# Parts of two norms issued at other products, between mixer 1 and the last feed-forward block

## The chip, the cores and the metric

The kernel runs on one core of a Trainium2 chip. The metric is the device time of one execution in microseconds (us), lower is better. The median of three runs before the change is 2760.47 us (2759.29 to 2761.58).

The engines of the core are PE (TensorE, matrix products; its weight loads are listed apart as PEld), DVE (VectorE), ACT (ScalarE), POOL (GpSimd) and SP (SyncE, which here only issues transfers). Each works through its own queue of instructions in order.

## The reference

A two-layer backbone over 512 latent tokens and 256 context tokens, model width 1024. Each layer is a half feed-forward block, a token mixer, and another half feed-forward block; each block is modulated, gated and closed by a layer norm:

```python
def layer_norm(x, g, b):
    xf = x.astype(jnp.float32)
    mu = jnp.mean(xf, axis=-1, keepdims=True)
    var = jnp.mean(jnp.square(xf - mu), axis=-1, keepdims=True)
    return ((xf - mu) * lax.rsqrt(var + LN_EPS)).astype(x.dtype) * g + b
...
def swiglu(u, w_in, w_out):
    a, v = jnp.split(u @ w_in, 2, axis=-1)
    return (jax.nn.silu(a) * v) @ w_out
...
        h_lat = layer_norm(ALPHA * h_lat + m_lat[5] * y_lat, ln_g[i, 1], ln_b[i, 1])

        h_lat = ffn_sublayer(h_lat, m_lat[6], m_lat[7], m_lat[8], ffn_w_in[i, 1], ffn_w_out[i, 1], ln_g[i, 2], ln_b[i, 2])
```

The last two statements, in layer 1 (the second layer), are the place of this change: `y_lat` is the output of mixer 1 (windowed attention), the norm behind it is called `l4` in the kernel, and the feed-forward block behind that is called "1b". Context tokens are no longer computed there. The output of "1b" is the result.

## The kernel before

**Data.** Activations lie transposed: eight tiles `z[d]` of 128 channels by 512 tokens (tile 0 in `zspare` for a while). In this part of the program the tokens are worked in two groups of 256, group 0 (tokens 0 to 255) and group 1. Weights come from DRAM in float32 tiles `wr` (128x512), one transfer each on SP's queue. Products are exact to float32: a tile is split in a high part (`wh` by an ACT cast, L102; `uh`, `gh`, `woh` for activations) and a low part (`wl` by a POOL subtraction, L104; `ul`, `gl`, `wol`), and each product is three matmuls: high by high (L163), low by high (L165), high by low (L166).

**A norm.** `layer_norm` (L428 on) makes five parts: sums (adds the eight tiles on DVE L347 and on POOL, called `asl`, with DVE's running sum in the PSUM tile `pml`), mean (a matmul by a matrix of ones into `pml`, L442), centers (eight DVE subtractions, L364, then eight squares on ACT, L451, and their sums on DVE and POOL, L347), variance (four small matmuls into `pvl`, L467, then on DVE an addition, L472, the seed of a reciprocal root, L354, and three Newton steps of three operations each, L357 to L359, that end in `yl`) and spreading (PE matmuls that spread `yl` over the tile, into `prl`, L395). Behind them come the outputs: per tile the norm itself (DVE, L480), then the modulated input of the next block, `ufl` (ACT L317), its high part `uh` (ACT L319) and low part `ul` (DVE L322). Last, "kept": POOL scales each tile for the residual (L335). So `l4[g]` is the list [sums, mean, centers, variance, spreading, outputs, kept] of group g.

**Products around it.** `wo_pairs` (L828) makes mixer 1's output products `pow`, eight tiles d per group, each evacuated by one DVE operation, z[d] += gate times product (`accumulate`, L495). The names `pow3_1_256_d` are those of the last head pairs' product for group 1. In `ffn` the first chunk of "1b" makes per group four products: `pa1b_0`, `pv1b_0`, `pa1b_1`, `pv1b_1` (each 8 tiles x 3 matmuls), a gate on each pair (`sl1b`, Silu on ACT, L522; times `pv1b` on DVE, L523; high part `gh1b` on ACT, L524; low part `gl1b` on DVE, L525), and then the eight down products `pd1b_0..7`, each 6 matmuls, each again evacuated by L495. All this is done for group 0 and then for group 1. Group 0's first products need the outputs of `l4[0]`; the norm of group 1 is done while group 0's products run. Behind this chunk come further chunks (with sums `x1b` of activations, L563), and at the end the final norm of the two groups (`layer_norm_pe`, L399: squares `sqfin` on ACT L412, sums `pvfin` on PE L414; outputs `ot` on ACT L1340 or POOL L1338, each stored by a transfer).

**Order.** A scheduler puts the instructions on each engine's queue by a modelled timeline, taking the program's own order into account. The program names points: `at("pa1b_0_0_0")` is reached just behind the code of that product, and `plan(point=[parts])` says which parts are issued there. `behind(x, y)` forces x to stand after y on the same engine; `accumulate` puts every evacuation behind `keep_back[0]`, if it is set.

## Time and profile before

| | |
|---|---|
| median of the runs | 2760.47 us |
| profiled execution | 2773.53 us |
| its span, first to last instruction | 2771.7 us |
| mean granted TensorE clock | 0.985 |
| ACT busy | 1204.9 us (43%) |
| POOL busy | 1674.3 us (60%) |
| DMA moved, mean | 113 GB/s |

The profile is of one execution, which is 13 us longer than the median of the runs. A timeline row reads: start in us, busy time in us, engine, line of the kernel, operation, outputs<-inputs, shape, how many such instructions in a row, and in brackets how long the engine had idled and which instruction released it. Buffer numbers are left out of names, so `z` can be any of tiles 1 to 7.

### The profile page before, as it was taken

To read this page: it belongs to the slowest core of one execution; us is meant where nothing else is said; L and a number is where in the kernel's file an instruction comes from. 1 tells how busy PE (TensorE), PEld (TensorE's weight loads), DVE (VectorE), ACT (ScalarE), POOL (GpSimd) and SP (SyncE) were. 2 spreads that over 40 slices of the span, in tenths; PEclk is the share of its full clock that TensorE was granted. 3 is DMA by queue.
4 is the path that set the end of the run, shared out by engine and by line. 5 is a ranking of instruction groups with operands and counts; after the bars stand their busy time and mean duration, and the time that the engine had idled before them with its cause. 6 is when DMAs were issued, how large, how long until landed. Compare 5 with 4: busy or idle time off the path is not lost. (4 is left out here: it accounts for less than half of the span.)

```text
span 2771.7 us, 47917 instructions
## 1 busy us (share of the span) xinstructions
PE 2659.9 (96%) x16954; PEld 2423.5 (87%) x16954; DVE 1857.4 (67%) x4250; ACT 1204.9 (43%) x2493; POOL 1674.3 (60%) x1522
## 2 busy tenths in 40 slices
PE   8999999999999989999999999999998999899997
PEld 5899998888888889999998899999986777898997
DVE  4877777775555677656565776666587667677765
ACT  5334343366446344343433434343336655444442
POOL 4786765464434556867664577767545445667762
PEclk9999999999999999999999999999998999999998
DMA  9367555422222213444453236465722111235551
GB/s 320 105 174 205 143 155 152 144 80 61 58 58 57 63 46 92 117 127 126 125 132 106 73 87 165 112 166 165 205 87 63 32 31 47 63 103 126 133 143 57
DMA packets 295615, 311.92 MB, mean 113 GB/s; under 512 B 27856, under 2 KB 193872, under 8 KB 294352
## 3 DMA queue, kind: packets, MB, share of 16 engines
q1 hardware_dynamic: 278960, 279.36, 33.8%
q0 software_dynamic: 16128, 29.37, 6.3%
q8 instruction: 134, 2.20, 0.3%
q14 instruction: 105, 0.86, 0.1%
q10 hardware_dynamic: 288, 0.14, 0.0%
HBM read 300.92 MB, written 12.25 MB: 113 GB/s over the span
## 5 line engine op out<-in xcount | busy, mean ns | idle before, releaser
L104 POOL TENSOR_TENSOR wl<-wr,wh 128x512 fp32r<-128x512 f32 x200 | 262.7, 1332 | 161.2 <-ACT wh L102 102.7
L104 POOL TENSOR_TENSOR wl_s<-S,wh_s 128x512 fp32r<-128x512 f32 x240 | 316.6, 1354 | 53.5 <-ACT wh_s L102 53.0
L102 ACT CAST wh_s<-S 128x512 fp32r<-128x512 f32 x256 | 155.9, 620 | 430.3 <-POOL S L636 151.2
L636 POOL TENSOR_TENSOR S<-wr,wr 128x512 f32<-128x512 f32 x128 | 173.6, 1356 | 191.8 <-DMA wr<-in_wst_dram 177.5
L211 DVE CUSTOM_DVE_ANT_0 jk<-wt,cb 128x512 f32<-128x512 f32 x360 | 244.5, 679 | 23.7 <-DMA wt<-in_wmodt_dram 18.9
L104 POOL TENSOR_TENSOR wl_a<-wr,wh_a 128x512 fp32r<-128x512 f32 x144 | 189.5, 1364 | 17.9 <-ACT wh_a L102 14.0
L102 ACT CAST wh_a<-wr 128x512 fp32r<-128x512 f32 x192 | 118.9, 622 | 152.8 <-PE pd1b L165 21.8
L102 ACT CAST wh<-wr 128x512 fp32r<-128x512 f32 x200 | 120.3, 617 | 85.5 <-DMA wr<-in_wst_dram 21.9
L495 DVE SCALAR_TENSOR_TENSOR z<-pd0b,gt,z 128x256 f32<-128x256 f32 (+1 forms) x168 | 97.0, 594 | 43.9 <-PE pd0b L166 43.2
L495 DVE SCALAR_TENSOR_TENSOR z<-pd1a,gt,z 128x512 f32<-128x512 f32 (+1 forms) x160 | 95.5, 613 | 39.1 <-PE pd1a L166 38.5
L912 POOL TENSOR_SCALAR p<-p,l 128x512 f32<-128x512 f32 x64 | 44.5, 697 | 110.0 <-DVE l L1020 107.5
L495 DVE SCALAR_TENSOR_TENSOR z<-pd0a,gt,z 128x512 f32<-128x512 f32 (+1 forms) x160 | 93.4, 611 | 16.5 <-PE pd0a L166 16.3
L335 POOL TENSOR_SCALAR z<-z,ag_None,ab_None 128x256 f32<-128x256 f32 (+1 forms) x78 | 62.7, 807 | 63.7 <-DVE uh L321 48.8
L636 POOL TENSOR_TENSOR S<-wr,S 128x512 f32<-128x512 f32 x64 | 90.4, 1413 | 3.5
L636 POOL TENSOR_TENSOR S<-S,wr 128x512 f32<-128x512 f32 x64 | 90.3, 1411 | 2.9
L912 POOL TENSOR_SCALAR pw<-pw,l 128x512 f32<-128x512 f32 (+1 forms) x64 | 41.2, 643 | 66.7 <-DVE l L1214 25.7
L1019 ACT ACTIVATE p<-s,m 128x512 f32<-128x512 f32 x64 | 44.0, 689 | 81.2 <-DVE m L1017 76.5
L317 ACT ACTIVATE ufl<-z,bi_None,sc_None 128x256 f32<-128x256 f32 (+1 forms) x86 | 55.3, 654 | 52.9 <-DVE z L480 51.8
L322 DVE TENSOR_TENSOR ul<-ufl,uh 128x256 fp32r<-128x256 f32 (+1 forms) x88 | 61.0, 699 | 5.1 <-ACT uh L319 3.6
L495 DVE SCALAR_TENSOR_TENSOR z<-pd1b,gt,z 128x512 f32<-128x512 f32 (+1 forms) x91 | 53.2, 618 | 11.2 <-PE pd1b L166 10.4
L211 DVE CUSTOM_DVE_ANT_0 jk<-zspare,cb 128x512 f32<-128x512 f32 x88 | 59.7, 678 | 0.5
L163 PE MATMUL vn<-wh,uh 128*128 128x256 f32 x192 | 54.9, 286 | 1.0 <-DVE nq L856 0.5
(1483 smaller groups left out, 10650.8 us busy)
## 6 DMA issues: line engine op xcount, KB each, us to landing
wr<-in_wst_dram SPq DMA_DIRECT2D x456, 256.0 KB
wt<-in_wmodt_dram SPq DMA_DIRECT2D x206, 256.0 KB
zspare<-in_wmodt_dram SPq DMA_DIRECT2D x50, 256.0 KB
wr_0b<-in_wst_dram SPq DMA_DIRECT2D x47, 256.0 KB
wr_1b<-in_wst_dram SPq DMA_DIRECT2D x47, 256.0 KB
wr_2b<-in_wst_dram SPq DMA_DIRECT2D x47, 256.0 KB
wr_3b<-in_wst_dram SPq DMA_DIRECT2D x47, 256.0 KB
wm<-in_wmod_dram SPq DMA_DIRECT2D x8, 1024.0 KB
```

The lines of the kernel that those rows point to most:

```text
L102: nc.scalar.copy(hi[:], src[:])
L104: x = eng.tensor_tensor(out=lo[:], in0=src[:], in1=hi[:].bitcast(F32), op=ALU.subtract)
L163: behind(nc.tensor.matmul(ps, a[0], b[0], start=first, stop=False), in_front[0])
L211: x = nc.vector.tensor_tensor_reduce(out=junk[:], in0=w[:], in1=cb[st], scale=1.0, scalar=0.0, op0=ALU.mult, op1=ALU.add, accum_out=out[st])
L317: nc.scalar.activation(uf[:, :n], zs, AF.Identity, scale=s1, bias=s2)
L322: return hi, nc.vector.tensor_tensor(out=lo, in0=uv, in1=uo.bitcast(F32), op=ALU.subtract)
L335: nc.gpsimd.tensor_scalar(out=zs, in0=zs, scalar1=prm[2][:, d:d + 1], scalar2=prm[3][:, d:d + 1], op0=ALU.mult, op1=ALU.add)
L495: last[0] = nc.vector.scalar_tensor_tensor(out=zt(d, c0, c1), in0=pd, scalar=gt[:, d, st:st + 1], in1=zt(d, c0, c1), op0=ALU.mult, op1=ALU ...
L636: nc.gpsimd.tensor_tensor(out=t[:], in0=a[:], in1=b[:], op=o)
L912: nc.gpsimd.tensor_scalar(out=p, in0=p, scalar1=r, scalar2=0.0, op0=ALU.mult, op1=ALU.add)
L1019: last_exp[0] = nc.scalar.activation(p[:], ps[:], AF.Exp, bias=m[:, 0:1], scale=-1.0, accum_out=l[:, 0:1])
```

## The change

No instruction is added or removed. Three things are edited:

1. The helper `back`, which sets `keep_back[0]`, moves out of `ffn` to the outer level.
2. When the variance of `l4[0]` has been issued (point `wo7_3`), `keep_back` is set to the last instruction of its Newton steps, and it is cleared again at point `pow3_1_256_2`. So the evacuations of products 0, 1 and 2 of group 1's last output products are forced behind the Newton steps of group 0's norm.
3. In the norm of group 1, mean and centers move from the point `pv1b_0_0_0` to `pa1b_0_0_0` (one product sooner, behind "kept" of group 0); variance moves from the down product 3 to `pv1b_0_1_0` (the last product ahead of the down products); spreading, outputs and "kept" move from down product 7 to down product 3.

```diff
     last_rstd, last_add, hold, keep_back = [None], [None], [None], [None]
+
+    def back(x):
+        keep_back[0] = x
...
-        def back(x):
-            keep_back[0] = x
...
-    plan(wo6_2=l4[0][:1], wo6_3=l4[0][1:2], wm7_3=l4[0][2:3], wo7_3=l4[0][3:4], pow3_1_256_2=l4[0][4:6],
-         pow3_1_256_7=l4[1][:1])
+    plan(wo6_2=l4[0][:1], wo6_3=l4[0][1:2], wm7_3=l4[0][2:3], wo7_3=l4[0][3:4] + [lambda: back(last_rstd[0])],
+         pow3_1_256_2=[lambda: back(None)] + l4[0][4:6], pow3_1_256_7=l4[1][:1])
     wa_mixer(gate(1, 5, 1.0))
-    plan(pa1b_0_0_0=l4[0][6:], pv1b_0_0_0=l4[1][1:3], pd1b_0_0_3=l4[1][3:4], pd1b_0_0_7=l4[1][4:])
+    plan(pa1b_0_0_0=l4[0][6:] + l4[1][1:3], pv1b_0_1_0=l4[1][3:4], pd1b_0_0_3=l4[1][4:])
     ffn("1b", g1, lambda: gate(1, 8, 0.5), None, final, apart=True)
```

Lines of the changed kernel behind L345 are 3 higher than before as far as L813, and 1 higher from there on; the rows below carry each kernel's own.

What the scheduler makes of it is seen in three places. First DVE's queue around the Newton steps of the first norm. A row is line, operation, output<-inputs, shape; `pow_1_256_d` is output product d of group 1. Before, from the second Newton step on (one step's start and an evacuation stand just ahead):

```order
L357 TENSOR_TENSOR pvl_0_26140<-pvl_0_26140,yl_0_26144 128x2
L495 SCALAR_TENSOR_TENSOR z_94<-pow_1_256_3_26235,gt_5_22846,z_94 128x256
L495 SCALAR_TENSOR_TENSOR z_95<-pow_1_256_4_26243,gt_5_22846,z_95 128x256
L358 SCALAR_TENSOR_TENSOR pvl_0_26140<-pvl_0_26140,yl_0_26144 128x2
L495 SCALAR_TENSOR_TENSOR z_96<-pow_1_256_5_26251,gt_5_22846,z_96 128x256
L359 SCALAR_TENSOR_TENSOR yl_0_26144<-pvl_0_26140,yl_0_26144 128x2
L495 SCALAR_TENSOR_TENSOR z_97<-pow_1_256_6_26259,gt_5_22846,z_97 128x256
L357 TENSOR_TENSOR pvl_0_26140<-pvl_0_26140,yl_0_26144 128x2
L358 SCALAR_TENSOR_TENSOR pvl_0_26140<-pvl_0_26140,yl_0_26144 128x2
L495 SCALAR_TENSOR_TENSOR z_98<-pow_1_256_7_26267,gt_5_22846,z_98 128x256
L359 SCALAR_TENSOR_TENSOR yl_0_26144<-pvl_0_26140,yl_0_26144 128x2
L347 TENSOR_TENSOR pml_1_26275<-z_95,z_96 128x256
```

and with the change:

```order
L360 TENSOR_TENSOR pvl_0_26140<-pvl_0_26140,yl_0_26144 128x2
L361 SCALAR_TENSOR_TENSOR pvl_0_26140<-pvl_0_26140,yl_0_26144 128x2
L498 SCALAR_TENSOR_TENSOR z_94<-pow_1_256_3_26235,gt_5_22846,z_94 128x256
L362 SCALAR_TENSOR_TENSOR yl_0_26144<-pvl_0_26140,yl_0_26144 128x2
L360 TENSOR_TENSOR pvl_0_26140<-pvl_0_26140,yl_0_26144 128x2
L361 SCALAR_TENSOR_TENSOR pvl_0_26140<-pvl_0_26140,yl_0_26144 128x2
L362 SCALAR_TENSOR_TENSOR yl_0_26144<-pvl_0_26140,yl_0_26144 128x2
L498 SCALAR_TENSOR_TENSOR zspare<-pow_1_256_0_26158,gt_5_22846,zspare 128x256
L498 SCALAR_TENSOR_TENSOR z_92<-pow_1_256_1_26166,gt_5_22846,z_92 128x256
L498 SCALAR_TENSOR_TENSOR z_93<-pow_1_256_2_26174,gt_5_22846,z_93 128x256
L498 SCALAR_TENSOR_TENSOR z_96<-pow_1_256_5_26251,gt_5_22846,z_96 128x256
L483 TENSOR_TENSOR zspare<-zspare,prl_0_26182 128x256
```

The three steps stand together, with only the evacuation of product 3 among them; products 0, 1, 2 and 5 are evacuated behind them, then come norm tiles of the first norm (L483, before L480), and the sums of the second norm (`pml` from z_95 and z_96) stand further back.

Second, PE's queue at the same place: the end of the output products and the spreading `prl`. Before:

```order
L163 MATMUL pow_1_256_7_26267<-woh_0_25512,wh_3_25536 128x256
L165 MATMUL pow_1_256_7_26267<-wol_0_25513,wh_3_25536 128x256
L166 MATMUL pow_1_256_7_26267<-woh_0_25512,wl_3_25537 128x256
L163 MATMUL pow_1_256_7_26267<-woh_1_25514,wh_3_25536 128x256
L165 MATMUL pow_1_256_7_26267<-wol_1_25515,wh_3_25536 128x256
L166 MATMUL pow_1_256_7_26267<-woh_1_25514,wl_3_25537 128x256
L395 MATMUL prl_0_26182<-idn,yl_0_26144 128x128 x2
L163 MATMUL pa1b_0_0_26364<-uh_101,wh_0_26290 128x256
```

and with the change:

```order
L163 MATMUL pow_1_256_5_26251<-woh_0_25512,wh_2_25530 128x256
L165 MATMUL pow_1_256_5_26251<-wol_0_25513,wh_2_25530 128x256
L166 MATMUL pow_1_256_5_26251<-woh_0_25512,wl_2_25531 128x256
L163 MATMUL pow_1_256_5_26251<-woh_1_25514,wh_2_25530 128x256
L165 MATMUL pow_1_256_5_26251<-wol_1_25515,wh_2_25530 128x256
L166 MATMUL pow_1_256_5_26251<-woh_1_25514,wl_2_25531 128x256
L398 MATMUL prl_0_26182<-idn,yl_0_26144 128x128 x2
L163 MATMUL pow_1_256_4_26243<-woh_0_25512,wh_2_25530 128x256
L165 MATMUL pow_1_256_4_26243<-wol_0_25513,wh_2_25530 128x256
L166 MATMUL pow_1_256_4_26243<-woh_0_25512,wl_2_25531 128x256
```

Product 5 is done ahead of product 4, the spreading of `yl` stands behind product 5 instead of behind product 7, and products 4, 7 and 6 follow it in this order, directly ahead of `pa1b`.

Third, DVE's queue at the gate of "1b" in group 0: last `ul` of the first norm, gate products, centers of the second norm. Before:

```order
L322 TENSOR_TENSOR ul_116<-ufl_0_7_26231,uh_108 128x256
L523 TENSOR_TENSOR pv1b_0_0_26397<-pv1b_0_0_26397,sl1b_0_0_26454 128x256
L364 TENSOR_TENSOR zspare<-zspare,pml_1_26275 128x256
L364 TENSOR_TENSOR z_92<-z_92,pml_1_26275 128x256
L364 TENSOR_TENSOR z_93<-z_93,pml_1_26275 128x256
L364 TENSOR_TENSOR z_94<-z_94,pml_1_26275 128x256
L364 TENSOR_TENSOR z_95<-z_95,pml_1_26275 128x256
L364 TENSOR_TENSOR z_96<-z_96,pml_1_26275 128x256
L364 TENSOR_TENSOR z_97<-z_97,pml_1_26275 128x256
L364 TENSOR_TENSOR z_98<-z_98,pml_1_26275 128x256
L525 TENSOR_TENSOR gl1b_0_26361<-pv1b_0_0_26397,gh1b_0_26360 128x256
L523 TENSOR_TENSOR pv1b_1_0_26484<-pv1b_1_0_26484,sl1b_1_0_26509 128x256
```

and with the change, from the sixth center on:

```order
L367 TENSOR_TENSOR z_96<-z_96,pml_1_26275 128x256
L367 TENSOR_TENSOR z_97<-z_97,pml_1_26275 128x256
L367 TENSOR_TENSOR z_98<-z_98,pml_1_26275 128x256
L526 TENSOR_TENSOR pv1b_0_0_26429<-pv1b_0_0_26429,sl1b_0_0_26454 128x256
L526 TENSOR_TENSOR pv1b_1_0_26484<-pv1b_1_0_26484,sl1b_1_0_26525 128x256
L350 TENSOR_TENSOR pml_1_26275<-pml_1_26275,sql_1_4_26416 128x256
L350 TENSOR_TENSOR pml_1_26275<-pml_1_26275,sql_1_5_26419 128x256
L528 TENSOR_TENSOR gl1b_0_26361<-pv1b_0_0_26429,gh1b_0_26360 128x256
L350 TENSOR_TENSOR pml_1_26275<-pml_1_26275,sql_1_6_26422 128x256
L528 TENSOR_TENSOR gl1b_1_26363<-pv1b_1_0_26484,gh1b_1_26362 128x256
L350 TENSOR_TENSOR pml_1_26275<-pml_1_26275,aql_1_0_26406 128x256
```

The gate product of the first pair (L523, now L526) stood ahead of the eight centers and stands behind them now, next to that of the second pair; the low parts `gl1b` (L525, now L528) follow after two sums of squares.

On PE, `pml` (the mean) has ten matmuls of the first four products behind it instead of eight; the four small `pvl` matmuls stand behind down product 1 instead of 3; `prl` of the second norm stays behind down product 7. On ACT the cast of one weight tile (of down product 6 and 7) comes behind `uh` 1 instead of ahead of `ufl` 0, the six squares of tiles 0 to 5 come ahead of the first `gh1b`, and in group 1 two weight casts come earlier while the two `sl1b` stand behind later casts; there `ul` 7 stands two DVE operations earlier. In the final norm, where nothing was planned anew, the last two `sqfin` squares of group 1 pass ahead of output rows `ot` on ACT.

## The prediction

> **What bounds the kernel now.** I read the page first: TensorE (PE) is busy 96% of the span and no other engine comes near, so only time in which PE stands still, or runs at half clock, can be won.

> ```profile
> PE 2659.9 (96%) x16954; PEld 2423.5 (87%) x16954; DVE 1857.4 (67%) x4250; ACT 1204.9 (43%) x2493; POOL 1674.3 (60%) x1522
> ```

> All that the diff moves is issued between mixer 1's last output products and the second group's first products of ffn 1b, some 2356 to 2410 us of the trace, so next three stretches there (columns: stretch, its length, busy time of PE, its weight loads, DVE, ACT, POOL, then granted clock, DMA share, GB/s).

> ```profile
> 2365.00:2379.00 14.00, 13.66 (x99) 13.35 (x99) 7.13 (x19) 9.56 (x20) 7.06 (x10) 0.88 0.11 28
> 2379.00:2393.00 14.00, 10.98 (x57) 9.63 (x56) 9.88 (x33) 3.12 (x9) 1.45 (x2) 0.76 0.01 1
> ...
> 2410.00:2440.00 30.00, 30.00 (x253) 30.00 (x253) 18.75 (x40) 12.37 (x31) 22.54 (x20) 1.00 0.34 101
> ```

> In the first the clock falls to 0.88, in the second to 0.76, and there PE also idles 3 us of 14. From 2410 on it is always busy, so a microsecond saved before should arrive at the end. The waits of PE from 2340 to 2440 say for what (sum, times, longest):

> ```profile
> PE pa1b L163 <- ACT uh L319: 4.2, 2, 2.5
> PE pd1b L165 <- DVE gl1b L525: 1.9, 2, 1.8
> PE prl L395 <- DVE yl L359: 1.6, 2, 0.9
> ```

> These are the two norms' chains (A the first group's, B the second's), and the gate between them. The clock follows a grid of 3.41 us:

> ```profile
> 2361.75:2365.16 3.41, 0.71 (x4) 0.52 (x4) 3.04 (x7) 1.19 (x3) 3.41 (x5) 1.00 0.58 163
> 2365.16:2368.57 3.41, 3.23 (x14) 3.09 (x15) 3.25 (x9) 3.41 (x8) 3.16 (x6) 0.50 0.41 111
> ...
> 2378.79:2382.20 3.41, 1.63 (x10) 1.12 (x9) 3.31 (x11) 2.79 (x9) 1.45 (x2) 1.00 0.00 0
> 2382.20:2385.61 3.41, 3.10 (x13) 2.50 (x13) 2.51 (x7) 0.54 (x2) 0.00 (x0) 0.50 0.00 0
> 2385.61:2389.02 3.41, 3.41 (x18) 3.41 (x17) 1.46 (x5) 0.00 (x0) 0.00 (x0) 0.50 0.02 5
> 2389.02:2392.43 3.41, 2.47 (x20) 2.23 (x19) 2.81 (x12) 0.00 (x0) 0.00 (x0) 1.00 0.00 0
> 2392.43:2395.84 3.41, 1.77 (x13) 1.58 (x14) 2.21 (x7) 2.25 (x5) 0.87 (x2) 1.00 0.00 0
> ```

> A step with 4 or 10 matmuls is followed by one at 0.50; after 20 or 13 the clock stays at 1.00. At half clock matmuls follow each other every 0.21 us, else every 0.12, so a slow step that PE fills costs 3.41 x 0.09 / 0.21 = 1.5 us. One slow step with 14 matmuls was enough to recover, one with 13 was not.

> **The change, part by part.** No instruction is added or removed, only places in the queues move. The profiled execution took 2773.53 us against a median of 2760.47; I work out differences in the profile and subtract them from the median.

> *A, the first norm.* On DVE the Newton steps were threaded between evacuations of the last products:

> ```profile
> 2357.12 0.15 DVE L354 TENSOR_SCALAR yl<-pvl 128x2 int32<-128x2 int32 x1
> 2357.30 0.17 DVE L357 TENSOR_TENSOR pvl<-pvl,yl 128x2 f32<-128x2 f32 x1
> ...
> 2361.88 0.15 DVE L359 SCALAR_TENSOR_TENSOR yl<-pvl,yl 128x2 f32<-128x2 f32 x1
> 2361.94 1.43 DVE L347 TENSOR_TENSOR pml<-z,z 128x256 f32<-128x256 f32 x1
> ...
> 2363.75 0.41 DVE L480 TENSOR_TENSOR zspare<-zspare,prl 128x256 f32<-128x256 f32 x1
> ```
> ```profile
> 2365.34 0.58 PE L163 MATMUL pa1b<-uh,wh 128*128 128x256 f32 x1 [2.55 <-ACT uh L319]
> ...
> 2378.80 0.28 PE L166 MATMUL pv1b<-uh,wl 128*128 128x256 f32 x1
> ```

> From seed to last step 4.91 us passed. In the changed order only the evacuation of product 3 stands between them; ten small operations some 0.2 us apart (first two rows) and one evacuation, 0.4, make about 2.55, so the last step ends near 2359.7 instead of 2362.03. The first norm tile (L480) stood behind that step and, for 1.81 us more (2361.94 to 2363.75), behind two sums of the other group. The sums now stand behind three norm tiles. I place `prl` at 2359.9, the tile at 2361.2 (evacuations of products 0, 1, 2 and 5, 0.4 apart, come first), and with the same 1.6 from tile to product the first product at 2363.0 instead of 2365.34: 2.3 earlier. What is late next: PE cannot start product 5 before product 3 is evacuated (new, about 0.6 idle at 2358.5), products 4, 7, 6 need the banks of 0, 1, 2, and `ul` 0 waits behind the 1.43 sum, to about 2364.6. From there the group's remaining 93 matmuls x 0.12 end near 2376.15 instead of 2378.80 + 0.28, that is 2.9 sooner: 1.4 of shorter chain and 1.5 of a slow step that should not come, since no step keeps fewer than about 18 matmuls. Below, were the slow step still there, 1.4; above 3.0.

> *B, the gate and the second norm.* Before, DVE did one gate product between `pml` and eight centers, the low part after them:

> ```profile
> 2381.25 0.39 PE L165 MATMUL pd1b<-gl1b,wh 128*128 128x256 f32 x1 [1.76 <-DVE gl1b L525]
> ...
> 2392.41 0.68 PE L395 MATMUL prl<-idn,yl 128*128 128x128 f32 x4 [0.94 <-DVE yl L359]
> 2394.73 0.39 PE L163 MATMUL pa1b<-uh,wh 128*128 128x256 f32 x1 [1.64 <-ACT uh L319]
> ```
> ```profile
> 2377.80 0.43 DVE L523 TENSOR_TENSOR pv1b<-pv1b,sl1b 128x256 f32<-128x256 f32 x1 [5.15 <-ACT sl1b L522]
> 2378.14 0.41 DVE L364 TENSOR_TENSOR zspare<-zspare,pml 128x256 f32<-128x256 f32 x1
> 2378.47 2.40 DVE L364 TENSOR_TENSOR z<-z,pml 128x256 f32<-128x256 f32 x7
> 2380.78 0.41 DVE L525 TENSOR_TENSOR gl1b<-pv1b,gh1b 128x256 fp32r<-128x256 f32 x1
> ```

> `pml` has ten matmuls behind it in the group instead of eight, 0.24 us, but the eight centers now stand ahead of both gate products. Centers from 2375.0 (2378.1 before, less 2.9 and 0.2) to 2377.8 (8 x 0.34), two gate products 0.7, two sums 0.7, `gl` 0.41: ready at 2379.7. PE has nothing from 2376.15 but two hi products near 2378.9: it stands still about 3.3 us, where it stood 1.8 plus pieces. That waiting is the price of this part, 1.3 us. The step it falls in has some 6 matmuls, so I expect half clock from 2378.8 to 2385.6 (as two steps of before). In 5.9 us at half clock, less 1.2 for `pvl` and small gaps, 22 of the 48 down products pass, 26 more take 3.1: the last ends near 2388.9 instead of 2391.48. What is won is the variance: it is taken after product 1, the Newton steps are over before product 6 is evacuated, and `prl` no longer waits its 0.94. From `prl` to the second group's first product took 2.32; that makes 2391.2 against 2394.73, 3.5 sooner, of which A holds 2.9. So B is **+0.6**. Bounds: without a second slow step 0.6 + 1.5 = +2.1; if other runs have no slow steps here before (ten matmuls against thirteen is near the edge) but have them after, -1.2.

> [...]

> *C, the second group's first products.* `ul` 7 stands two DVE operations earlier, which ends most of PE's wait for it; but the gate's `sl1b` now stands behind weight casts on ACT, of which one waited for its transfer:

> ```profile
> 2406.09 0.38 PE L165 MATMUL pa1b<-ul,wh 128*128 128x256 f32 x1 [1.15 <-DVE ul L322]
> ```
> ```profile
> 2408.82 0.63 ACT L102 CAST wh<-wr 128x512 fp32r<-128x512 f32 x1 [1.81 <-DMA wr<-in_wst_dram]
> ```

> The first row's wait and 0.2 behind it bound the gain at 1.35; a transfer as late as the second row's leaves nothing. I take the middle, **0.7**.

> *Tail.* In the final norm two squares pass ahead of output rows on ACT:

> ```profile
> 2754.42 1.08 ACT L1340 ACTIVATE ot<-z,lnp_sb 128x256 f32<-128x256 f32 x2
> 2755.40 0.40 ACT L412 ACTIVATE sqfin<-z 128x256 f32<-128x256 f32 x1
> ...
> 2759.12 0.60 ACT L1340 ACTIVATE ot<-z,lnp_sb 128x256 f32<-128x256 f32 x1 [1.35 <-DMA out_dram<-ot]
> ```

> The last square comes 1.3 sooner, and PE's last sum waited for it; but an output row waits for an earlier row's transfer, which does not move. 0.4 to 1.3, taken as **0.8**.

> Sum: 2.9 + 0.6 + 0.7 + 0.8 = 5.0 us, 2760.5 - 5.0 = **2755.5**. Bounds of the parts: 1.4 - 1.2 + 0 + 0.4 = 0.6 and 3.0 + 2.1 + 1.35 + 1.3 = 7.75.

> **Rivals.** (1) *Slower: half clock that holds.* PE's longer wait in B, 3.3 us, could keep the clock down past two steps, through the rest of the down products (26 x 0.09 = 2.4) and the second group's first four products (4 x 8 tiles x 3 matmuls = 96, x 0.09 = 8.6). 2755.5 + 11.0 = 2766.5. It decides from the step at 2385.6: if that is at 0.50, this is it. Against it: the row at 2385.61 is the last slow one although PE was waiting just before. Chance 0.09.
> (2) *A is not won*: the bank waits and the late `ul` 0 hold the products, or the slow step only moves; A gives 0.5. 2755.5 + 2.4 = 2757.9. For it: the 1.43 sum is still there. Chance 0.14.
> (3) *Absorbed later*: products are sooner but weights are not; POOL, which makes the low parts of all weights, is busy 22.54 of 30.00 us from 2410 on, and a wait on it or on the loads would take the lead back. Then only the tail counts, 2759.7. Against it: PE's 30.00 of 30.00. Chance 0.13.
> (4) *No slow step in B*: the 22 matmuls that I put at half clock pass in 22 x 0.09 = 2.0 us less, 2753.5. [...] Chance 0.08.
> That the change does nothing is out: the queues of DVE and PE differ in the order shown.

> **How the numbers follow.** The forecast has 0.56. About 0.2% (5.5 us: 2754.95 and 2765.99) is what a measurement of this kernel can tell from no change, and the forecast lies 0.5 inside it: I give its part beyond 0.22, its part inside 0.34. Faster is 0.22 + 0.08 = 0.30; same 0.34 + 0.14 + 0.13 = 0.61; slower 0.09. The range runs from 2752.2, most of the way to the parts' upper bound, to 2760.2, behind rival 3; it leaves out rival 1 and the ends, some 0.15.

> **What would show it.** A: the yl of L359 (after: L362) within 2.7 us of its seed, `uh` 0 some 2 us sooner, clock 1.00 in the step after the first `prl`. B: PE waiting over 2.5 us for `gl1b`, two steps at 0.50, no wait of the second `prl` for yl. C: no wait of `pa1b` for `ul` near 2403. Tail: last `pvfin` a microsecond sooner relative to the first. Wrong if the clock at 2386 is still 0.50, if group 0's products end less than 1.5 us sooner, or if the lead at 2395 is gone at 2530.

## The result, and the profile after

The changed kernel is a little faster. Thirteen runs gave a median of 2752.72 us against 2759.83 us for the kernel before, a ratio of 0.9976 (95% interval 0.9967 to 0.9986). It was measured twice more, on other occasions: 0.9993 (0.9981 to 1.0005) and 0.9971 (0.9955 to 0.9987). Weighted by their intervals the three give 0.9980, with some 0.0007 to either side: **5.4 us, between 3.5 and 7.3**. The three differ by a little more than their intervals allow, so these bounds are rather too narrow. A kernel with the old order, measured in the same way, gave 0.9999 (0.9988 to 1.0011). A single comparison of this size is thus not worth much, and the traces have to carry the parts.

The profiled execution of after is 18.4 us shorter in span (2753.3 against 2771.7), but 12.8 us of that stand already where the end of mixer 1 begins, ahead of everything that the change touches. So the spans say nothing; lengths between two instructions that both kernels have do. I use five stretches: the end of **mixer** 1 (from the first of its last 32 matmuls `wo` to the seed of the first norm), **A** (from there to the start of group 0's last `pv1b`), **B** (to group 1's first product), **C** (to the next chunk's first product `p11b`), and the **final norm** (to the end). Below, in this order, the windows view of the kernel before (length, busy time of PE, its weight loads, DVE, ACT, POOL, granted clock, DMA share, GB/s):

```profile
2351.17:2357.12 5.95, 4.33 (x52) 3.52 (x48) 2.94 (x9) 2.00 (x5) 0.54 (x1) 1.00 0.00 0
2357.12:2378.80 21.68, 18.49 (x135) 17.70 (x135) 14.20 (x43) 12.55 (x24) 13.45 (x15) 0.92 0.19 50
2378.80:2394.73 15.93, 11.27 (x60) 9.72 (x58) 11.19 (x38) 4.46 (x13) 1.45 (x2) 0.79 0.00 1
2394.73:2449.88 55.15, 52.36 (x432) 51.75 (x433) 40.83 (x89) 26.07 (x59) 43.21 (x42) 1.00 0.32 92
2727.07:2771.72 44.65, 28.81 (x210) 27.27 (x208) 24.81 (x79) 13.53 (x31) 3.66 (x6) 0.80 0.14 48
```

and the same of the changed kernel's first profile:

```profile
2338.41:2345.37 6.96, 5.34 (x51) 4.39 (x48) 2.93 (x8) 1.99 (x5) 0.53 (x1) 0.80 0.00 0
2345.37:2367.33 21.96, 20.51 (x136) 19.45 (x136) 14.46 (x43) 12.91 (x25) 13.38 (x15) 0.83 0.19 49
2367.33:2380.45 13.12, 9.12 (x60) 8.28 (x58) 10.88 (x37) 4.10 (x12) 1.45 (x2) 0.87 0.01 1
2380.45:2432.45 52.00, 51.87 (x432) 51.67 (x433) 39.65 (x89) 26.38 (x59) 43.12 (x42) 1.00 0.33 97
2709.03:2753.27 44.24, 29.01 (x210) 27.64 (x208) 24.84 (x79) 13.59 (x31) 3.64 (x6) 0.80 0.15 48
```

B is 2.8 shorter, C 3.2, the end 0.4. A, which was to give most, is 0.3 longer, and its clock is 0.83: the first of three slow steps in a row begins before the seed, in matmuls of mixer 1 that the change does not touch. The steps of the clock's grid there, and around the gate:

```profile
2339.20:2342.61 3.41, 1.79 (x20) 1.17 (x17) 1.98 (x4) 1.00 (x2) 0.00 (x0) 1.00 0.00 0
2342.61:2346.03 3.42, 3.42 (x25) 3.09 (x21) 0.96 (x6) 0.37 (x1) 0.00 (x0) 0.50 0.00 0
2346.03:2349.44 3.41, 2.83 (x13) 2.54 (x13) 2.03 (x10) 1.24 (x2) 2.07 (x2) 0.50 0.00 0
2349.44:2352.85 3.41, 3.41 (x18) 3.41 (x17) 2.58 (x7) 0.97 (x2) 1.38 (x3) 0.50 0.56 154
2352.85:2356.27 3.42, 2.69 (x20) 2.29 (x19) 2.83 (x8) 3.42 (x8) 3.42 (x4) 1.00 0.29 69
2366.51:2369.92 3.41, 1.10 (x10) 0.90 (x8) 3.34 (x11) 2.75 (x9) 1.45 (x2) 1.00 0.00 0
2369.92:2373.33 3.41, 3.36 (x14) 3.06 (x15) 2.63 (x8) 0.96 (x3) 0.00 (x0) 0.50 0.00 0
2373.33:2376.75 3.42, 3.42 (x28) 3.27 (x28) 2.98 (x14) 0.00 (x0) 0.00 (x0) 1.00 0.00 0
```

```profile
PE pd1b L163 <- ACT gh1b L527: 2.3, 1, 2.3
PE pa1b L163 <- ACT uh L319: 1.6, 1, 1.6
...
PE pow L163 <- DVE z L498: 0.6, 1, 0.6
PE pa1b L165 <- DVE ul L322: 0.4, 1, 0.4
```

The 2.55 for the first `uh` and both waits for `yl` are gone; the gate's wait has grown to 2.3 and ends on `gh1b`, whose cast stands behind the gate product on DVE, which now follows the eight centers, and behind six squares on ACT.

### The profile page after: what moved, and what is told of

Same layout as the page of the kernel before. It is cut to its first block, busy times and chain, and to the rows that moved or that the text cites. A ratio compares the mean times of both kernels' runs of the same rounds, so it can differ in the third digit from the quotient of the medians.

```text
span 2753.3 us, 47923 instructions
## 1 busy us (share of the span) xinstructions
PE 2649.0 (96%) x16954; PEld 2415.1 (88%) x16954; DVE 1843.1 (67%) x4250; ACT 1204.3 (44%) x2493; POOL 1673.9 (61%) x1522
## 5 line engine op out<-in xcount | busy, mean ns | idle before, releaser
L102 ACT CAST wh_s<-S 128x512 fp32r<-128x512 f32 x256 | 155.8, 621 | 430.6 <-POOL S L639 161.7
L102 ACT CAST wh_a<-wr 128x512 fp32r<-128x512 f32 x192 | 119.0, 621 | 152.1 <-PE pd1b L165 21.0
L102 ACT CAST wh<-wr 128x512 fp32r<-128x512 f32 x200 | 120.3, 617 | 86.8 <-DMA wr<-in_wst_dram 21.5
L322 DVE TENSOR_TENSOR ul<-ufl,uh 128x256 fp32r<-128x256 f32 (+1 forms) x88 | 60.9, 698 | 3.7 <-ACT uh L319 2.2
L163 PE MATMUL vn<-wh,uh 128*128 128x256 f32 x192 | 54.9, 286 | 0.9 <-DVE nq L857 0.6
```

What stands on the lines that cost most here:

```text
L102: nc.scalar.copy(hi[:], src[:])
L163: behind(nc.tensor.matmul(ps, a[0], b[0], start=first, stop=False), in_front[0])
L322: return hi, nc.vector.tensor_tensor(out=lo, in0=uv, in1=uo.bitcast(F32), op=ALU.subtract)
```

## The experiments

All were run with a profile and compared with the kernel before on the same chip. Lengths of the five stretches in us, from the windows view, with the slow clock steps that lie between the end of mixer 1 and C's end:

| kernel | mixer | A | B | C | final norm | slow steps | ratio to before |
|---|---|---|---|---|---|---|---|
| before | 5.95 | 21.68 | 15.93 | 55.15 | 44.65 | 1 in A, 2 in B | |
| before, again | 7.04 | 22.64 | 15.12 | 54.98 | 44.67 | 2 from mixer, 1 each in A, B, C | 0.9999 |
| changed | 6.96 | 21.96 | 13.12 | 52.00 | 44.24 | 3 from mixer, 1 in B | 0.9976 |
| changed, again | 7.08 | 21.98 | 14.54 | 52.18 | 44.10 | 3 from mixer, 2 in B | 0.9993 |
| changed, third | 5.95 | 19.44 | 12.31 | 52.42 | 44.55 | none | 0.9971 |
| Newton steps only | 5.95 | 19.43 | 13.20 | 55.11 | 44.57 | none | 0.9993 |
| second norm only | 5.95 | 21.63 | 13.44 | 53.09 | 44.57 | 1 in A, 2 in B | 0.9990 |
| centers late | 5.95 | 19.43 | 13.18 | 55.08 | 44.57 | none | 0.9992 |
| centers only | 5.95 | 19.45 | 15.84 | 53.45 | 45.10 | 2 in B, 1 in C | 0.9998 |
| changed + matmuls | 5.95 | 19.44 | 12.33 | 51.68 | 44.09 | none | 0.9972 |
| the same, again | 7.21 | 21.97 | 12.33 | 52.20 | 45.07 | 3 from mixer | 0.9967 |
| before + matmuls | 7.19 | 21.53 | 14.75 | 52.31 | 44.58 | 2 from mixer, 2 in B | 0.9983 |
| Newton steps of both | 5.95 | 19.46 | 11.40 | 52.90 | 44.19 | none | 0.9976 |
| `ul` ahead | 7.03 | 22.89 | 15.01 | 54.78 | 44.66 | 2 from mixer, 1 each in A, B, C | 1.0007 |

Some of the expectations below count differently: A to the end of group 0's last `pv1b` (22.0 in the kernel before), and the final norm only as far as its last spreading `prfin` (32.8 in the kernel before).

**Newton steps only.** The second norm's line of the plan is the old one:

```diff
-    plan(pa1b_0_0_0=l4[0][6:] + l4[1][1:3], pv1b_0_1_0=l4[1][3:4], pd1b_0_0_3=l4[1][4:])
+    plan(pa1b_0_0_0=l4[0][6:], pv1b_0_0_0=l4[1][1:3], pd1b_0_0_3=l4[1][3:4], pd1b_0_0_7=l4[1][4:])
```

> The changed kernel with the second norm's parts at their old points: only the evacuations behind the first Newton steps. If the parts add up (my theory), this has A and nothing else: seed of the first norm (L357) to the end of group 0's last pv1b, 22.0 us before, shorter by 2.4 to 2.9 at an equal number of slow clock steps; the second spreading still waits about 0.9 for yl; the total 2 to 3 us under before. If A is lost again behind (rival 2 of the prediction), the stretch is shorter by less than 1 and the total is within 1 us of before.

A is 2.25 shorter than in the profile before, C and the end are as before, and the second spreading still waits for `yl`. The timeline of PE:

```profile
2372.91 0.68 PE L398 MATMUL prl<-idn,yl 128*128 128x128 f32 x4 [0.74 <-DVE yl L362]
2375.22 0.38 PE L163 MATMUL pa1b<-uh,wh 128*128 128x256 f32 x1 [1.64 <-ACT uh L319]
```

The grid lies as in the profile before, within 0.1 us, yet A's slow step is gone: the new order itself avoids it here, and it is part of the 2.25. Ratio 0.9993 (0.9980 to 1.0006): the total can't tell 2 us from none.

**Second norm only.** The other half:

```diff
-    ... wo7_3=l4[0][3:4] + [lambda: back(last_rstd[0])],
-         pow3_1_256_2=[lambda: back(None)] + l4[0][4:6], ...
+    ... wo7_3=l4[0][3:4], pow3_1_256_2=l4[0][4:6], ...
```

> The changed kernel without the order behind the Newton steps: only the second norm's parts sooner. My theory: the stretch from seed to group 0's end stays at 22.0 us; from there to group 1's first product it falls from 15.7 to 13.5 to 15.0, by the slow steps it meets; group 1's first products run 1 to 2 us shorter; total 3 to 5 us under before. If the whole gain is made by the Newton steps (rival), the total is within 1 us of before.

The grid again lies as in the profile before. A stays at 21.6 with its slow step, B falls by 2.5 with as many slow steps as before, C by 2.1; ratio 0.9990 (0.9978 to 1.0002). So B and C come with the second norm's parts, A with the Newton steps.

**Centers late.**

```diff
-    plan(pa1b_0_0_0=l4[0][6:] + l4[1][1:3], pv1b_0_1_0=l4[1][3:4], ...
+    plan(pa1b_0_0_0=l4[0][6:], pv1b_0_0_0=l4[1][1:3], pv1b_0_1_0=l4[1][3:4], ...
```

> The changed kernel with mean and centers of the second norm back at the point one product later, variance and spreading kept sooner. My theory has the eight centers ahead of the gate products as the price of part B (1.3 us of PE's waiting): PE's wait at the first down product falls from 2.3 to 1.0 to 1.8, and the total is up to 1 us under the changed kernel. Rival: the early centers are what makes the variance early, so that the second spreading waits for yl again (0.5 to 1.0), and the total is 1 us over the changed kernel.

The gate's wait falls to 1.7, as my theory had it, but the wait for `yl` is back, 0.7, as the rival had it, and every stretch is that of the Newton steps alone, C's 55.1 included; ratio 0.9992 (0.9981 to 1.0003). Without sooner centers the sooner variance is worth nothing.

**Changed + matmuls.** In `down`, ahead of the first product of `pd1b_0`:

```diff
+                if pn == "pd1b_0_0_0":
+                    for _ in range(24):
+                        behind(nc.tensor.matmul(pd, rw(w, 0, 0, P)[0], uh[0][:, c0:c1], start=True, stop=True), last_pe[0])
```

> The changed kernel with 24 further matmuls (128x256, of tiles that lie there, into the bank of the first down product, which overwrites them) while PE waits for the gate. If a slow step follows a step with few matmuls (my theory), the step behind the gate runs at 1.00, the 48 down products pass in some 6.5 us instead of 8.3, and the total is 1 to 1.5 us under the changed kernel. [...]

Run twice; the second time beside the changed kernel:

> The changed kernel with 24 added matmuls in the gate's wait, once more, beside the changed kernel on the same chip. My theory: no slow step behind the gate, 12.3 us from group 0's end to group 1's first product, against 13.1 with one slow step and 14.5 with two; the total 1 to 2 us under the changed kernel's on that chip. Rival: the same total within 0.5 us.

Both have B at 12.33 and no slow step in it. The rival is that the grid's place did this and not the matmuls. In the second run it may have: a step begins 2.07 us behind the start of group 0's last `pv1b`, in the third profile of the changed kernel 2.12 behind it (counted on from the slow steps elsewhere in the trace), and that one has no slow step and a B of 12.31 without any added matmul. The first is the better witness. There the step begins 3.39 behind that matmul (which starts at 2366.35), and in "second norm only", which has the same plan for the second norm, 3.41 (behind 2374.79). The steps from the gate on, first of "second norm only", then of this run:

```profile
2374.78:2378.19 3.41, 0.79 (x5) 0.38 (x3) 3.31 (x11) 2.82 (x10) 1.46 (x2) 1.00 0.00 0
2378.19:2381.60 3.41, 3.13 (x15) 3.13 (x15) 2.56 (x7) 0.39 (x2) 0.00 (x0) 0.50 0.00 0
2381.60:2385.02 3.42, 3.42 (x17) 3.42 (x17) 2.44 (x13) 0.00 (x0) 0.00 (x0) 0.50 0.00 0
```
```profile
2366.32:2369.74 3.42, 3.38 (x29) 3.17 (x27) 3.32 (x11) 2.84 (x9) 1.49 (x2) 1.00 0.00 0
2369.74:2373.15 3.41, 3.29 (x25) 3.09 (x26) 3.15 (x11) 0.16 (x1) 0.00 (x0) 1.00 0.02 5
```

So by this one pair the added matmuls do keep the clock, and B is 12.33 instead of 13.44. Against the changed kernel's first two profiles it is 0.8 less than with one slow step and 2.2 less than with two. As a version it gave 0.9972 (0.9958 to 0.9987) and 0.9967 (0.9953 to 0.9981), with 0.9971 for the changed kernel beside the second: not to be told apart.

**Before + matmuls.** The same in the old order, 20 matmuls behind the first spreading, into a bank of their own:

```diff
+    def fill():
+        ps = bank("c", "fill")
+        for _ in range(20):
+            behind(nc.tensor.matmul(ps[:, 0:256], fill_of[0][0], fill_of[0][1], start=True, stop=True), prev_ln[0])
...
-         pow3_1_256_7=l4[1][:1])
+         pow3_1_256_7=l4[1][:1] + [fill])
```

> The kernel before with 20 further matmuls (128x256, into a bank of their own, not read) behind the first norm's spreading, where PE waits 2.55 us for uh. My theory has 1.5 us of part A as one slow clock step, the rest as a shorter chain. Then the stretch from seed to group 0's end falls from 21.7 to 20.2 to 20.4 without any change on DVE, and the total is about 1.5 us under before. If A is all chain (rival), the stretch stays at 21.7 or is longer by what the added matmuls delay (up to 0.3).

A is 21.53, not 20.2, since mixer 1's slow steps reach into it. Against the old order's second profile, which has the same beginning, it is 1.1 shorter, and the slow step 10.7 behind the seed is gone. By this one pair, that is the price of A's slow step. The rest of the run is not what was meant: the added matmuls shifted the scheduler's times, it put the second norm's Newton steps sooner by itself, and C fell to 52.31; the ratio of 0.9983 (0.9971 to 0.9994) holds both.

**Centers only.** Variance, spreading and outputs at the old points (`pd1b_0_0_3` and `pd1b_0_0_7`).

> The changed kernel with variance, spreading and outputs of the second norm at their old points; only its mean and centers are sooner. If the sooner centers are what lets the variance come early (as the run with late centers suggests), this has the cost of the centers (PE's first down product waits 2.3 or more) and, with the variance behind product 3, a wait of 0.5 to 1.0 at the second spreading; group 0's end to group 1's first product 14 to 15, total 1 to 2 us over the changed kernel. If only the centers' place counts, all is as in the changed kernel within 0.5 us.

The two waits are as expected, 2.3 at the gate and 0.9 at the second spreading. B, 15.84, is above the 14 to 15, with two slow steps. The changed kernel's second profile has two as well, its grid lies the same at the gate within 0.1 us, and its B is 14.54, so the sooner variance is worth 1.3 there. Ratio 0.9998 (0.9988 to 1.0009). C, less its slow step, is that of the changed kernel, so C hangs on the centers' place, not on the variance's.

**Newton steps of both norms.** On top of the added matmuls:

```diff
+    ... pd1b_0_0_2=[lambda: back(last_rstd[0])], pd1b_0_0_4=[lambda: back(None)] + l4[1][4:])
```

> The kernel with the added matmuls in the gate's wait, and the edit of the Newton steps made for the second norm too: the evacuations of down products 3 and 4 stand behind its Newton steps, so the spreading comes behind product 4 instead of 7 and the norm runs beside products 5 to 7. My theory (PE waits for the chain from spreading to uh): from the end of the down products to group 1's first product the 2.4 us of waiting fall to 0.5 to 1.2, and the stretch from group 0's end to group 1's first product from 12.3 to 10.8 to 11.5; total 1 us under the run with the added matmuls. Rival: the down products wait for their banks by as much; stretch 12.3 or more.

B is 11.40, 0.9 under the run without this; C gives 0.7 to 1.2 of it back in a wait of 1.0 for `ul`. The ratio, 0.9976 (0.9966 to 0.9985), does not show the 1 us that I expected over the run without it.

**Repetitions, and `ul` ahead.** The order before and the changed kernel for further profiles, and the order before with three sums of the next chunk forced behind the last `ul` of group 1:

> The changed kernel once more, for a second profile of it. If the three slow steps at the end of mixer 1 in its first profile come from where the clock's steps fell and not from the change, the stretch from seed to group 0's end is 19.4 with none of them, 21 to 22 with some; from there to group 1's first product 13.1 with one slow step, 12.3 with none; group 1's stretch 52.0 and the final norm 31.7 to 32.0 as in the first profile, since those do not hang on the clock. If these differ, they are no effect of the order.

> The kernel before with the helper moved and its old plan: the same order of instructions, for a second profile and as a measure of what a comparison of equals gives. Ratio to before 1.000 within 0.001. Group 1's stretch 55.1 and the final norm 32.7 to 32.8 as in the first profile, whatever the clock does; seed to group 0's end 20.2 with no slow step, 21.7 with one, more with the three at the end of mixer 1.

> The changed kernel a third time. The two earlier measurements stand at 0.9976 and 0.9993 of before; by the parts (2.2 to 2.9 for the Newton steps, 0.9 and more for the gate stretch, 3.1 for group 1's products, 0.4 for the end) I expect 0.9975 to 0.9985 here. Rival: the second measurement is the true one, and the ratio is 0.999 or more.

> The kernel before with one thing: three sums of the next chunk (x1b_0) stand behind the last low part ul of group 1 on DVE, so that ul comes sooner. Theory for group 1's stretch (55.1 before, 52.0 changed): two waits of PE make it, 1.1 to 1.3 for ul and 1.4 for an evacuation behind weight low parts. Then here the first goes and the second stays: stretch 53.7 to 54.1, total about 1.2 us under before. Rival: both waits have one cause, the stretch falls to 52.0 to 52.6. Other rival: the time comes back as a wait at the next place, 55.1.

The third measurement of the changed kernel, 0.9971, lies a little under the 0.9975 to 0.9985 that I expected, which its interval covers. Its profile meets the clock undisturbed:

```profile
2342.37:2348.32 5.95, 4.33 (x52) 3.52 (x48) 2.93 (x8) 1.99 (x5) 0.54 (x1) 1.00 0.00 0
2348.32:2367.76 19.44, 17.75 (x137) 16.47 (x135) 14.33 (x43) 12.82 (x25) 13.36 (x15) 1.00 0.19 56
2367.76:2380.07 12.31, 7.95 (x59) 6.99 (x57) 10.71 (x37) 4.11 (x12) 1.45 (x2) 1.00 0.00 1
2380.07:2432.49 52.42, 51.87 (x433) 51.67 (x434) 40.04 (x89) 26.33 (x59) 43.13 (x42) 1.00 0.33 96
```

The old order's second profile has the disturbed beginning:

```profile
2338.53:2345.57 7.04, 5.42 (x51) 4.47 (x48) 2.94 (x8) 1.99 (x5) 0.54 (x1) 0.79 0.00 0
2345.57:2368.21 22.64, 20.21 (x136) 19.57 (x136) 13.22 (x42) 12.64 (x24) 13.50 (x15) 0.84 0.17 48
```

So compare like with like: with mixer 1 undisturbed, A is 21.68 against 19.44, 2.2 gained; with it disturbed, 22.64 against 21.96 and 21.98, 0.7 gained. `ul` ahead settles nothing: both profiles of the old order with the disturbed beginning have a slow step at the start of C, PE is late there anyway, and neither shows the wait for `ul`; C is 54.78 against 54.98, the ratio 1.0007 (0.9993 to 1.0021).

## Why the prediction was right, and where not

The time, 2755.5 against 2752.72 and a weighted gain of 5.4 against 5.0, came out right, but its four terms did not; their errors cancelled, and that is luck. (The working also slips by 0.2: a tile at 2361.2 and 1.6 behind it make 2362.8, not 2363.0.)

**A, 2.9 forecast, 2.2 or 0.7 measured.** The chain was read rightly: from the seed to the spreading 4.96 became 2.74, in the third profile, where I had 2.78. Of DVE's queue in the first profile:

```profile
2345.37 0.15 DVE L357 TENSOR_SCALAR yl<-pvl 128x2 int32<-128x2 int32 x1
...
2347.74 0.48 DVE L498 SCALAR_TENSOR_TENSOR z<-pow,gt,z 128x256 f32<-128x256 f32 x1 [1.21 <-PE pow L166]
2348.14 0.15 DVE L362 SCALAR_TENSOR_TENSOR yl<-pvl,yl 128x2 f32<-128x2 f32 x1
...
2348.72 0.16 DVE L362 SCALAR_TENSOR_TENSOR yl<-pvl,yl 128x2 f32<-128x2 f32 x1
```

Here the one evacuation that stands among the steps waited 1.21 for a product that PE made at half clock, so the last step ends 3.5 behind the seed, not 2.6: that is how a slow step ahead of A takes A's gain. The term that failed is "1.5 of a slow step that should not come, since no step keeps fewer than about 18 matmuls". I counted steps at one place of the grid. Where the grid is as in the profile before, the step does stay away, and is worth 1.1. Where it is not, slow steps come from mixer 1, and the change adds one to them. The 0.6 of new waiting for product 3 was there, as forecast, but where it fell into a slow step, another followed. In the old order's second profile the step at that place is full, and the next runs at 1.00:

```profile
2346.07:2349.49 3.42, 3.42 (x18) 3.42 (x18) 2.13 (x8) 1.24 (x2) 1.92 (x2) 0.50 0.00 0
2349.49:2352.90 3.41, 2.64 (x21) 2.25 (x20) 2.88 (x12) 1.24 (x2) 3.41 (x5) 1.00 0.52 136
```

In the changed kernel (2346.03 in the steps further up) it holds 13 matmuls in 2.83 us, and the next is at 0.50 again. All three profiles of the changed order with the disturbed beginning have three slow steps there, all three of the old order two. A count of matmuls alone does not tell it either: the step from 2339.20 has 20, of 128 columns instead of 256, and half clock follows. The prediction had named as a sign of being wrong "if group 0's products end less than 1.5 us sooner": counted from the seed, that is so in the first two profiles and not in the third.

**B, 0.6 forecast, 0.9 measured between profiles without slow steps (13.20 with the Newton steps only, 12.31 with the whole change), 2.2 between the means with them.** Right: the price (the first low-part product stands 3.4 behind group 0's end instead of 2.45, 1.0 for my 1.3) and the gain (the spreading waits no more). What failed is "half clock from 2378.8 to 2385.6 (as two steps of before)": the three profiles of the changed kernel have one, two and none (mean of B 13.3), the old order's two and one (15.5). Where the two came as forecast, in the second profile, B is 14.54, still 1.4 under before: the rest of the stretch was forecast too long as well. That PE waits for `gl1b` was wrong in the name only; it waits for `gh1b`, which is cast on ACT from the gate product. DVE and ACT in the first profile:

```profile
2368.76 0.76 DVE L526 TENSOR_TENSOR pv1b<-pv1b,sl1b 128x256 f32<-128x256 f32 x2
2369.43 0.96 DVE L350 TENSOR_TENSOR pml<-pml,sql 128x256 f32<-128x256 f32 x2
2370.30 0.41 DVE L528 TENSOR_TENSOR gl1b<-pv1b,gh1b 128x256 fp32r<-128x256 f32 x1
```
```profile
2369.22 0.42 ACT L454 ACTIVATE sql<-z 128x256 f32<-128x256 f32 x1
2369.54 0.35 ACT L527 CAST gh1b<-pv1b 128x256 fp32r<-128x256 f32 x1
```

The first gate product is done some 0.4 us behind 2368.76, so the squares hold up the cast by 0.4 at most; the rest of the wait is the centers'. And the centers are not only its price, as I had it: they make the variance early.

**C, 0.7 forecast, 2.6 to 3.1 measured.** I had sized it by the wait for `ul` and took half. That wait went whole in all three profiles. The larger miss is a second wait, which I passed over as "from 2410 on it is always busy": from 2441.97 on, just behind that window, PE stood still 1.44 us in the old order for an evacuation. In the timelines of the kernel before, PE, then ACT and DVE:

```profile
2443.41 0.39 PE L163 MATMUL pd1b<-gh1b,wh 128*128 128x256 f32 x1 [1.44 <-DVE z L495]
```
```profile
2436.75 0.37 ACT L597 CAST T1b_3h<-x1b_o 128x256 fp32r<-128x256 f32 x1 [2.00 <-DVE x1b_o L563]
2437.02 1.14 ACT L102 CAST wh_a<-wr 128x512 fp32r<-128x512 f32 x2
2438.07 1.14 ACT L102 CAST wh_s<-S 128x512 fp32r<-128x512 f32 x2
2439.11 0.37 ACT L524 CAST gh1b<-pv1b 128x256 fp32r<-128x256 f32 x1
```
```profile
2439.51 0.42 DVE L525 TENSOR_TENSOR gl1b<-pv1b,gh1b 128x256 fp32r<-128x256 f32 x1 [1.20 <-ACT gh1b L524]
2439.85 2.45 DVE L104 TENSOR_TENSOR wl_a<-wr,wh_a 128x512 fp32r<-128x512 f32 x2
...
2442.89 1.25 DVE L495 SCALAR_TENSOR_TENSOR z<-pd1b,gt,z 128x256 f32<-128x256 f32 x3
```

DVE waits for `gh1b`, then makes two low parts of weights, 2.45 (POOL does not make those of all weights, though the prediction says so), then two sums, and only then evacuates. In the changed kernel ACT does one of the weight casts while it waits for `x1b_o`:

```profile
2418.66 0.62 ACT L102 CAST wh_a<-wr 128x512 fp32r<-128x512 f32 x1 [0.15 <-PE pv1b L165]
2419.85 0.37 ACT L600 CAST T1b_3h<-x1b_o 128x256 fp32r<-128x256 f32 x1 [0.56 <-DVE x1b_o L566]
```

`gh1b` and all behind it come sooner, and the wait is 0 to 0.5. This swap, far behind the edited lines, stands in every profile with sooner centers and in the one with matmuls added to the old order; the wait of 1.4 or 1.5 stands in every profile without it (before twice, Newton steps only, centers late, `ul` ahead). That the swap alone makes the 1.4 was not tried by itself.

**Final norm, 0.8 forecast, 0.1 to 0.6 measured.** The last square came 0.9 sooner counted from the first, where I had 1.3, and the output rows on POOL waited for a transfer, the cover that I had named (in the first profile they start at 2743.26, released by `out_dram<-ot`, and one on ACT waits 0.87 for such a transfer). The gain is not clear of the spread: "changed + matmuls" has the same order in the final norm in both runs and took 44.09 and 45.07. In the second the clock falls to half 24.6 us behind the start of the final norm, in the first 27.7.

**The rivals.** Half clock that holds (1) didn't come: from mixer 1 to C's end the clock was back after three steps at most. A not won (2) holds in part, where mixer 1 ends disturbed, and by what it names: the wait for product 3's bank, and a slow step that only moves (two and one of the old order become three and none). Absorbed later (3): in the first profile the lead at `p11b`, 17.4 us over the whole trace, is 18.0 at the start of the final norm, so this pair gives nothing back. It settles little: from `p11b` to the final norm the fourteen profiles take 271.4 to 279.0 us, with an order that nobody planned anew, so whether the lead is kept rests on the times of the runs. No slow step in B (4) was one of three profiles; its chance of 0.08 was my estimate, and no row of before stood for it. The length of the wait does not decide it: in the first profile it was 2.33 us, and the step behind it ran at 0.50; in the third it was 2.3, and the clock stayed at 1.00. The kernel before has a step in which the trace shows no wait over 0.34 us, and half clock follows even there:

```profile
1013.47:1016.89 3.42, 2.55 (x17) 2.04 (x17) 2.79 (x11) 0.37 (x1) 0.11 (x1) 1.00 0.01 2
1016.89:1020.30 3.41, 3.41 (x16) 3.23 (x16) 2.54 (x11) 0.50 (x2) 0.00 (x0) 0.50 0.02 5
```

## What to carry to other kernels

Where a schedule comes from a modelled timeline, a small edit reorders queues far behind it, and that can be worth more than the edit: before pricing it, list every wait of the bottleneck engine as far as the last row that moved, not only up to the next busy window. A term that rests on slow clock steps was priced here at one place of the grid, where A gained 2.2 us, and at another A gained 0.7; price such a term for several, and compare stretches only between profiles in which the grid lies alike at their start. A move that looks like a price (here the centers ahead of the gate) should be taken back alone before it is called one.

## What the hardware showed that I had not expected

Where the clock's grid fell made as much of a difference as the change did: A of the changed order is 19.44 us with mixer 1 undisturbed and 21.96 and 21.98 with it disturbed, 2.5 apart, and the change was worth 2.2 or 0.7 there. The same instructions at mixer 1's end took 5.95 us in eight profiles and 6.96 to 7.21 in six, and in those six two or three slow steps follow. Read from the slow steps of each trace, a grid step begins 0.5 to 0.8 us behind the start of that stretch in all six, and at 0.2 to 0.5 or 1.4 to 1.5 us in the eight others. One slow step cost 0.6 to 1.1 us in the pairs above, not the 1.5 that I had for one that PE fills; that PE waits for others in part of it is my reading, not tried by itself (PE was busy 2.83 of 3.41 us in the one from 2346.03 of the changed kernel). And 24 matmuls whose result nobody reads kept the next step at 1.00 where, with the grid within 0.02 us of the same place, a step with 5 matmuls was followed by two slow ones.
